# Other homes for the buffers of a hybrid encoder layer: mixer, output projection and MLP on one core of Trainium2

## The chip, the core and the metric

The kernel runs on one core of one Trainium2 chip. The metric is device microseconds of one launch on that core; the time before is the median of 3 runs. The core has five engines that run side by side, each with its own queue of instructions: TensorE (PE in the rows) multiplies matrices out of SBUF into eight PSUM banks, VectorE (DVE), ScalarE (ACT) and GpSimd (POOL) work on tiles of up to 128 partitions, and SyncE (SP) here issues all the DMA transfers between HBM and SBUF.

## The reference, cut to what matters

One encoder layer over T = 2048 tokens of width 1024, in float32, with 256 memory tokens:

```
h = rmsnorm(x, norm_mix_w)
q, k, v, z, xbc, dt, qx = split(h @ w_in)      # 512, 128, 128, 1024, 1536, 32, 512 columns
att  = windowed_gqa(rope(rmsnorm(q)), rope(rmsnorm(k)), v, sink)   # 8 heads, 2 kv, +-128 tokens
xbc  = silu(conv5(xbc)); y = ssd(forward) + ssd(backward) + d * xs # 16 heads, chunks of 128
ssd  = rmsnorm(y * silu(z)) per group                              # 2 groups of 512
xatt = cross_attention(rmsnorm(qx), mem @ w_mem_kv)                # 4 heads
x = x + concat(att, ssd, xatt) @ w_out
return x + square(relu(rmsnorm(x, norm_mlp_w) @ w_up)) @ w_down    # inner width 4096
```

## The kernel before, in words

**Products.** A float32 operand is split into two numbers of TensorE's faster float type, hi and lo (`split`: ACT makes hi, DVE or POOL makes lo); a product is three matmuls, hi·hi, hi·lo and lo·hi. So every weight and every activation is loaded raw, split, and kept twice (names ending in h and l, in regions named X, W, A).

**Stages.** Stage 1 runs the tokens in two halves, 1024 to 2047 first ("half one"), then 0 to 1023 ("half two"). In each: `kv_products` loads xT (the transposed x, 8 blocks k of 128 rows), splits it and multiplies by w_kvdt (288 columns) for eight token tiles of 128; then the 12 xbc columns with their convolution, cross attention in four pairs of tiles, and q in four pairs, whose results are transposed in A and stored to q_d. In half two the backward SSD states ("back chunks") lie between them. `z_first` ends stage 1: the eight columns of z for the first 512 tokens. Stage 2 goes over 16 token tiles times 2 groups: an attention unit, an SSD unit and, for the other tokens, one of 24 z columns (`z_col`, 24 matmuls each), with `z_block` loading and splitting xT again for every 512 tokens. Stage 3 takes pairs of tiles through the output projection (`out_pair`: four products of 4 blocks of 128 rows of w_out each) and `mid` (norm, transposes, sums stored to xc_d), and then the MLP, written as seven products of half matrices instead of eight (`ORDER`), weights loaded into wr0 and wr1, combined, and split into wh and wl.

**What sets the order.** The program records all instructions, then `plan()` orders them by a cost model: it keeps the ready instructions of each engine by their place in the recording, takes the engine that can start first (on equal times the first in the list `engs`), hands out the eight PSUM banks, lets eight DMAs be in flight, and lets DVE and POOL use their shared SBUF port one at a time (`port`). The engines' queues are then issued in that order, all from line 390 (391 after the change), so every row has that line; tiles tell the instructions apart.

**Homes.** SBUF is divided into named regions: const, late, small, X0 to X3, W0, W1, A0, A1, B, Z, C, E. `use(region, ...)` gives a region a new set of buffers; each name in it is a ring of so many buffers. Nothing in the new set may be written before every user of the region's previous set is done, whichever of its buffers that was. `memory1()` to `memory4()` are these maps for stage 1, stage 2, the output projection and the MLP. A row's names are regions: `X<-xbc_d` is a load from DRAM into one of X0 to X3.

Of the kernel before, what the change touches and what calls it, by code (L numbers as in the profile page):

```python
# [73 lines left out]
class Program:  # L74
# [193 lines left out]
    def plan(self):  # L268

        engs = ("", "PE", "ACT", "DVE", "POOL", "SP")  # L270
# [131 lines left out]
class Memory:  # L402
# [5 lines left out]
    def use(self, region, dt, **tags):  # L408

        size = {t: -(-n // CELL) * CELL for t, (n, _) in tags.items()}  # L410
        total = sum(size[t] * b for t, (_, b) in tags.items())
# [4 lines left out]
        for t, (_, b) in tags.items():  # L416
            self.tags[t] = (v, at, size[t], b, dt)
            self.count[t] = 0
            at += size[t] * b
# [15 lines left out]
class Hybrid:  # L435
# [53 lines left out]
    def constants(self):  # L489
# [28 lines left out]
        self.load(cols, a["cols"])  # L518
# [33 lines left out]
    def memory1(self):  # L552
# [8 lines left out]
        m.use("B", F32, pre=(1030, 2), cacc=(1026, 2), stg=(1024, 2), tm=(512, 3), bbt=(256, 2))  # L561
        m.use("Z", F32, raw=(1024, 2), rrow=(1024, 1), vd=(160, 1), rp_u=(128, 1))
        m.use("C", F32, state=(1024, 2), vm=(1024, 1), rp_w=(128, 1))

    def memory2(self):
        m = self.mem
        m.use("X0", F32R, zxh=(512, 8))
        m.use("X1", F32R, zxl=(512, 8))
        m.use("A0", F32R, zwh=(1024, 2), zwl=(1024, 2))
        m.use("Z", F32, zwr=(1024, 1), zraw=(512, 2), zrow=(512, 1), zt=(512, 2))  # L570
        m.use("A1", F32R, sr=(1024, 2), kw=(768, 2))
        m.use("E", F32R, mv=(1024, 2), qs=(512, 2))
        m.use("X2", F32, xb=(1536, 2), y=(512, 2))
        m.use("X3", F32, ap=(1536, 2), ao=(256, 2))
        m.use("W0", F32, fr=(1024, 2), bk=(1024, 2))
        m.use("W1", F32, pb=(1024, 2), ee=(1024, 2))
        m.use("B", F32, xs=(1280, 2), sf0=(512, 2), sf1=(512, 2), apT=(1536, 2))
        m.use("C", F32, vw=(192, 2), zth=(512, 2), xw=(512, 2))

    def memory3(self):  # L580
        m = self.mem
        for i, (h, l) in enumerate((("X0", "X1"), ("late", "A1"), ("X2", "X3"), ("W0", "W1"))):
            m.use(h, F32R, **{f"woh{i}": (1024, 4)})
            m.use(l, F32R, **{f"wol{i}": (1024, 4)})
        m.use("A0", F32R, ah=(512, 4), al=(512, 4))
# [5 lines left out]
    def memory4(self):  # L591
        m = self.mem
        m.use("X0", F32R, xr0=(2048, 2))
        m.use("X1", F32R, xr1=(2048, 2))
# [124 lines left out]
    def kv_products(self, pool, t0, tts, w, ps):  # L719

        nc, a = self.nc, self.a
        if not w:
            self.xh, self.xl = [], []
        rings = ("cacc", "cacc", "pre", "pre", "stg", "stg", "cacc", "cacc")
# [409 lines left out]
    def z_first(self, pool):  # L1134
# [167 lines left out]
    def stage2(self):  # L1302
# [337 lines left out]
def layouts(inp):  # L1640
# [61 lines left out]
```

## Time and profile before

| what | value |
|---|---|
| median of 3 runs | 2861.55 us (2851.22 to 2866.41) |
| profiled execution | 2861.82 us, span 2859.8 us |
| busy share of the span | PE 97%, DVE 66%, ACT 48%, POOL 19% |
| mean granted clock of TensorE | 0.989 |
| chain that ended last | PE 81%, DVE 6%, DMA 6%, ACT 4% |
| DMA | 510.27 MB, mean 178 GB/s |

The span runs from the first to the last instruction. An engine's busy share says how much of the span it worked, not whether it was late; the chain says who held up the end, step by step. TensorE's idle time, 2859.8 less 2760.0, is short and lies in few places, so the rows below look at stretches: where its busy time is less than the stretch, and where the clock that it was granted is below 1.00. In a timeline row the bracket at the end is the idle time before it and what released it.

### The profile page before, as it was taken

The page shows a single profiled execution, that of the slowest core. Times are in us where ns is not written, and L with a number is a line of the kernel's source. Part 1 is how long each engine was busy: PE and PEld are TensorE (multiplying, and loading weights), DVE is VectorE, ACT ScalarE, POOL GpSimd, SP SyncE. Part 2 cuts the span into 40 slices and gives each one's busy share as a digit, 9 for nine tenths or more (in the row PEclk, how much of TensorE's full clock was granted, in tenths as well). Part 3 has the DMA queues.
Part 4 walks back from the last instruction along what each step waited for, and adds up shares of the span by engine and source line. Part 5 has one row for each costly group of instructions (what it writes and reads, how often), then busy time and mean ns, then how long its engine had stood idle before and what let it go on. Part 6 is the DMA issues. An engine that isn't in the chain of part 4 may idle for free.

```text
span 2859.8 us, 37348 instructions
## 1 busy us (share of the span) xinstructions
PE 2760.0 (97%) x13628; PEld 2254.6 (79%) x13628; DVE 1899.3 (66%) x3115; ACT 1359.1 (48%) x2276; POOL 544.7 (19%) x488
## 2 busy tenths in 40 slices
PE   8999979999889999999999899999999999999999
PEld 7788767787667777768888788888888888888887
DVE  6874558855567766666767577584848585766756
ACT  5545534353457676663333363444435353535352
POOL 2302424426254544431101000000000000000000
PEclk9999989999999999999999999999999999999999
DMA  6561335634597877775555691726344653626251
GB/s 212 174 201 60 110 118 170 192 100 155 190 293 223 261 238 234 213 240 190 208 178 204 241 343 56 239 85 204 121 157 165 240 181 111 199 96 221 77 174 59
DMA packets 283691, 510.27 MB, mean 178 GB/s; under 512 B 35954, under 2 KB 124402, under 8 KB 283508
## 3 DMA queue, kind: packets, MB, share of 16 engines
q1 hardware_dynamic: 283508, 507.89, 54.1%
q8 instruction: 108, 1.77, 0.3%
q14 instruction: 75, 0.61, 0.1%
HBM read 390.36 MB, written 117.45 MB: 178 GB/s over the span
## 4 chain that ended last, share of the span: by engine, by line
PE 81%; DVE 6%; DMA 6%; ACT 4%; issue 2%; POOL 1%; SPq 0%; ACTq 0%; POOLq 0%; DVEq 0%
PE bank L390 81%; DVE B L390 2%; ACT X L390 2%; DVE X L390 1%; ACT B L390 1%; DVE small L390 1%; DVE A L390 1%; DMA Z<-in_x_dram 1%; ACT W L390 1%; DMA B<-in_xT_dram 1%; DMA Z<-in_w_out_dram 1%; ACT A L390 1%; POOL B L390 1%; DVE W L390 1%; POOL W L390 0%
## 5 line engine op out<-in xcount | busy, mean ns | idle before, releaser
L390 PE MATMUL bank<-X,X 128*128 128x512 f32 x2688 | 611.0, 389 | 2.0 <-DVE X L390 2.0
L390 PEld LDWEIGHTS bank<-X,X 128*128 128x128 f32 x2688 | 504.6, 188 | 106.9 <-DVE X L390 2.4
L390 PE MATMUL bank<-X,E 128*128 128x512 f32 x1792 | 551.7, 389 | 0.0
L390 PEld LDWEIGHTS bank<-X,E 128*128 128x128 f32 x1792 | 336.4, 188 | 69.8
L390 PE MATMUL bank<-X,W 128*128 128x512 f32 (+1 forms) x1584 | 367.0, 381 | 8.0 <-ACT W L390 3.1
L390 PE MATMUL bank<-X,A 128*128 128x512 f32 x1344 | 350.3, 406 | 11.8 <-ACT X L390 8.3
L390 PE MATMUL bank<-X,C 128*128 128x512 f32 x896 | 348.5, 389 | 0.0
L390 PEld LDWEIGHTS bank<-X,W 128*128 128x128 f32 x1584 | 286.3, 191 | 67.7 <-issue 6.0
L390 PEld LDWEIGHTS bank<-X,A 128*128 128x128 f32 x1344 | 249.4, 190 | 79.4 <-issue 15.0
L390 PE MATMUL bank<-W,X 128*128 128x512 f32 (+1 forms) x1152 | 253.5, 370 | 12.4 <-ACT X L390 11.3
L390 DVE TENSOR_TENSOR X<-A,X 128x1024 fp32r<-128x1024 f32 x128 | 156.5, 1222 | 122.3 <-ACT X L390 121.6
L390 PEld LDWEIGHTS bank<-W,X 128*128 128x128 f32 x1152 | 195.3, 192 | 43.3 <-ACT X L390 11.7
L390 DVE TENSOR_TENSOR X<-Z,X 128x1024 fp32r<-128x1024 f32 x100 | 123.1, 1232 | 135.1 <-ACT X L390 135.0
L390 DVE TENSOR_TENSOR B<-B,bank 128x512 f32<-128x512 f32 x286 | 189.9, 683 | 34.3 <-PE bank L390 34.1
L390 PEld LDWEIGHTS bank<-X,C 128*128 128x128 f32 x896 | 168.2, 188 | 34.8
L390 ACT CAST X<-A 128x1024 fp32r<-128x1024 f32 x128 | 134.0, 1047 | 117.0 <-PE bank L390 115.7
L390 DVE TENSOR_TENSOR W<-W,bank 128x512 f32<-128x512 f32 x220 | 145.2, 683 | 48.0 <-POOL W L390 25.8
L390 ACT ACTIVATE X<-X,small 128x384 f32<-128x384 f32 (+1 forms) x256 | 143.5, 601 | 62.9 <-DVE small L390 62.8
L390 ACT CAST X<-Z 128x1024 fp32r<-128x1024 f32 x100 | 105.0, 1051 | 132.9 <-PE bank L390 99.6
L390 ACT ACTIVATE W<-W 128x512 f32<-128x512 f32 x224 | 134.1, 627 | 59.8 <-DVE W L390 57.4
L390 POOL TENSOR_TENSOR W<-W 128x512 f32<-128x512 f32 x92 | 119.9, 1314 | 183.6 <-ACT W L390 161.3
L390 ACT CAST E<-W 128x1024 fp32r<-128x1024 f32 x66 | 69.3, 1051 | 166.3 <-PE bank L390 164.5
(169 smaller groups left out, 4031.0 us busy)
## 6 DMA issues: line engine op xcount, KB each, us to landing
X<-xc_d SPq DMA_DIRECT2D x112, 1024.0 KB
A<-in_w_up_dram SPq DMA_DIRECT2D x64, 512.0 KB
A<-in_w_down_dram SPq DMA_DIRECT2D x64, 512.0 KB
xc_d<-E SPq DMA_DIRECT2D x56, 512.0 KB
Z<-in_w_z_dram SPq DMA_DIRECT2D x32, 512.0 KB
W<-erow_d SPq DMA_DIRECT2D x64, 256.0 KB
Z<-in_w_xbc_dram SPq DMA_DIRECT2D x24, 512.0 KB
X<-xbc_d SPq DMA_DIRECT2D x16, 768.0 KB
```

Of the source, the lines that this page charges most:

```text
L390: o.fn(*[fix(x) for x in o.args], **{k: fix(x) for k, x in o.kw.items()})
```

## The change

It has six parts, none of which changes what is computed.

1. The port in turns: in `plan`, when DVE and POOL can start at the same time, the one that did not use the port last comes first.
2. The constants: the table `cols` is loaded in two pieces, the first without the cosines and sines (256 of its 368 columns).
3. Input in halves: `kv_products` loads and splits xT in blocks of 512 tokens instead of 1024, the first block ahead of the second; w_kvdt comes in pieces of 288, 576, 864 and 576 columns.
4. Stage 1 and 2 homes: `use` lets a buffer have a type of its own; zt, vd, bbt and the rope scratch leave B, C and part of Z; most of stage 2's buffers change region.
5. The output projection: ah and al go to X3, wol2 to A0.
6. The MLP: xr0, wr0, wh, wl, xr1, wr1 and us change region.

TensorE's and POOL's instructions are as many as before; the splits of xT are 16 of 512 columns instead of 8 of 1024 in each half, and the DMAs 1230 instead of 1211.

```diff
-        engs = ("", "PE", "ACT", "DVE", "POOL", "SP")
+        engs = ["", "PE", "ACT", "POOL", "DVE", "SP"]
...
             if o.port:
                 port = end
+                engs[3:5] = ("POOL", "DVE") if e == "DVE" else ("DVE", "POOL")
...
-        self.load(cols, a["cols"])
+        first = NCOL - 256
+        self.load(cols[:, :first], a["cols"][:, :first])
...
         yield
+        self.load(cols[:, first:], a["cols"][:, first:])
...
-        m.use("B", F32, pre=(1030, 2), cacc=(1026, 2), stg=(1024, 2), tm=(512, 3), bbt=(256, 2))
-        m.use("Z", F32, raw=(1024, 2), rrow=(1024, 1), vd=(160, 1), rp_u=(128, 1))
-        m.use("C", F32, state=(1024, 2), vm=(1024, 1), rp_w=(128, 1))
+        m.use("B", F32, pre=(1030, 2), cacc=(1026, 2), stg=(1024, 2), tm=(512, 3))
+        m.use("Z", F32, raw=(1024, 2), rrow=(1024, 1), zt=(512, 2))
+        m.use("E", F32, vd=(160, 1), rp_u=(128, 1), rp_w=(128, 1), bbt=(256, 2))
+        m.use("C", F32, state=(1024, 2), vm=(1024, 1))
 
     def memory2(self):
         m = self.mem
+        m.use("E", F32R, mv=(1024, 2), qs=(512, 2))
+        m.use("A1", F32R, sr=(1024, 2), kw=(768, 2), vw=(192, 2, F32))
+        m.use("A0", F32, fr=(1024, 2), xw=(512, 2), ao=(256, 2))
+        m.use("B", F32, xs=(1280, 2), sf0=(512, 2), sf1=(512, 2), xb=(1536, 2))
+        m.use("C", F32, ap=(1536, 2))
         m.use("X0", F32R, zxh=(512, 8))
         m.use("X1", F32R, zxl=(512, 8))
-        m.use("A0", F32R, zwh=(1024, 2), zwl=(1024, 2))
+        m.use("X2", F32, apT=(1536, 2), y=(512, 2))
+        m.use("X3", F32R, zwh=(1024, 2), zwl=(1024, 2))
+        m.use("W0", F32, bk=(1024, 2), pb=(1024, 2))
+        m.use("W1", F32, ee=(1024, 2), zth=(512, 2))
         m.use("Z", F32, zwr=(1024, 1), zraw=(512, 2), zrow=(512, 1), zt=(512, 2))
-        m.use("A1", F32R, sr=(1024, 2), kw=(768, 2))
-        m.use("E", F32R, mv=(1024, 2), qs=(512, 2))
-        m.use("X2", F32, xb=(1536, 2), y=(512, 2))
-        m.use("X3", F32, ap=(1536, 2), ao=(256, 2))
-        m.use("W0", F32, fr=(1024, 2), bk=(1024, 2))
-        m.use("W1", F32, pb=(1024, 2), ee=(1024, 2))
-        m.use("B", F32, xs=(1280, 2), sf0=(512, 2), sf1=(512, 2), apT=(1536, 2))
-        m.use("C", F32, vw=(192, 2), zth=(512, 2), xw=(512, 2))
...
-        for i, (h, l) in enumerate((("X0", "X1"), ("late", "A1"), ("X2", "X3"), ("W0", "W1"))):
+        for i, (h, l) in enumerate((("X0", "X1"), ("late", "A1"), ("X2", "A0"), ("W0", "W1"))):
...
-        m.use("A0", F32R, ah=(512, 4), al=(512, 4))
+        m.use("X3", F32R, ah=(512, 4), al=(512, 4))
...
-        m.use("X1", F32R, xr1=(2048, 2))
-        m.use("A0", F32, wr0=(1024, 4))
-        m.use("A1", F32, wr1=(1024, 4))
-        m.use("X2", F32R, wh=(1024, 4))
-        m.use("X3", F32R, wl=(1024, 4))
+        m.use("X1", F32, wr0=(1024, 4))
+        m.use("late", F32R, wh=(1024, 4))
+        m.use("A1", F32R, wl=(1024, 4))
+        m.use("X2", F32R, xr1=(2048, 2))
+        m.use("A0", F32, wr1=(1024, 4))
...
-        m.use("late", F32, us=(1024, 2))
+        m.use("X3", F32, us=(1024, 2))
...
+    def kv_weights(self, pool, w, n):
+
+        k = len(w)
+        if k % 3 == 0:
+            self.kv_piece = [pool.tile([P, 864], t, r) for t, r in ((F32, "raw"), (F32R, "wh"), (F32R, "wl"))]
+        s = slice(k % 3 * 288, (k % 3 + n) * 288)
+        raw, hi, lo = (t[:, s] for t in self.kv_piece)
+        self.load(raw, self.a["w_kvdt"][k // 3][:, s])
+        self.split(hi, lo, raw)
...
+    def kv_products(self, pool, t0, b, tts, w, ps):
...
+        load = len(self.x_in) < 2 * KT and b == len(self.x_in) // KT
...
+        sb = slice(b * BLK, (b + 1) * BLK)
         for k in range(KT):
+            if load:
+                if k % 2 == 0:
+                    raw2 = pool.tile([P, 1024], F32, ("cacc", "pre", "stg", "cacc", "pre", "stg", "cacc", "pre")[b * 4 + k // 2])
+                raw = raw2[:, (k % 2) * BLK:(k % 2 + 1) * BLK]
+                self.load(raw, self.a["xT"][k, :, t0 + b * BLK:t0 + (b + 1) * BLK])
             if len(w) <= k:
...
+                self.kv_weights(pool, w, 1 if k == 0 else 3 - k % 3 if k < 6 else 2)
+            if load:
+                self.split(self.xh[k][:, sb], self.xl[k][:, sb], raw, self.w_mix[:, k:k + 1])
+                self.x_in.append(k)
...
-            self.kv_products(pool, t0, range(0, 4), wk, pk)
+            self.x_in = []
+            self.kv_products(pool, t0, 0, range(0, 4), wk, pk)
...
+            self.kv_products(pool, t0, 1, (4, 5), wk, pk)
             w0 = self.weights(pool, a["w_xbc"][0], (KT, P))
...
+            self.kvdt_tiles(pool, t0, range(0, 4), pk)
             self.xbc_col(pool, t0, 0, w0)
-            self.kv_products(pool, t0, (4, 5), wk, pk)
-            self.kvdt_tiles(pool, t0, range(0, 4), pk)
-            self.kv_products(pool, t0, (6, 7), wk, pk)
+            self.kv_products(pool, t0, 1, (6, 7), wk, pk)
...
-            self.z_col(pool, 0, c, self.z_weights(pool, c, "w"), "stg")
+            self.z_col(pool, 0, c, self.z_weights(pool, c, "w"), self.r_row[:, BLK:])
...
-        for n, (ts, ring) in enumerate(((self.mv, "fr"), (self.sr, "bk"))):
+        for n, (ts, ring) in enumerate(((self.mv, "fr"), (self.sr, "fr"))):
```

In words for what is cut: `cols` has its parts in another order, so that the cosines and sines stand last; in `z_col` zt always comes from the ring zt and th, the tanh's buffer, from the caller.

Three places in the queues show what the orders make of it. First SyncE's queue where half one ends and half two begins. B is the region of xT's landing buffers, A_0 that of q's transposed results, Z that of raw weights. Before:

```order
L390 DMA q_d<-A_0_99 128x1024 x3
L390 DMA B_100<-in_xT_dram 128x1024
L390 DMA q_d<-A_0_99 128x1024
L390 DMA B_100<-in_xT_dram 128x1024
L390 DMA Z_101<-in_w_kvdt_dram 128x576
L390 DMA q_d<-A_0_99 128x1024
L390 DMA Z_101<-in_w_xbc_dram 128x1024
L390 DMA B_100<-in_xT_dram 128x1024 x2
L390 DMA Z_101<-in_w_xbc_dram 128x1024 x2
L390 DMA q_d<-A_0_99 128x1024
L390 DMA B_100<-in_xT_dram 128x1024
L390 DMA q_d<-A_0_99 128x1024
```

After; four more loads of 512 stand up to 12 rows further ahead:

```order
L391 DMA q_d<-A_0_99 128x1024 x3
L391 DMA B_100<-in_xT_dram 128x512 x2
L391 DMA q_d<-A_0_99 128x1024
L391 DMA B_100<-in_xT_dram 128x512
L391 DMA Z_101<-in_w_kvdt_dram 128x576
L391 DMA B_100<-in_xT_dram 128x512 x2
L391 DMA Z_101<-in_w_xbc_dram 128x1024
L391 DMA q_d<-A_0_99 128x1024
L391 DMA B_100<-in_xT_dram 128x512 x4
L391 DMA Z_101<-in_w_xbc_dram 128x1024
L391 DMA q_d<-A_0_99 128x1024
L391 DMA B_100<-in_xT_dram 128x512
```

Before, the seventh and the eighth load of xT stand behind the sixth and the seventh q_d store. Now the eighth half load (the last of tiles 0 to 3) stands ahead of the fifth q_d store, and the last of the second half, four rows below these, behind the seventh.

Second, TensorE's queue at the end of z_first, whose last matmul is the first row. A_1_5589 and, after, A_1_5699 hold sr and kw, E mv and qs; xb is X_1_5703 before and B_5611 after, and A_1_5039 holds the state product's other operand, xw. Before:

```order
L390 MATMUL bank_82<-X_0_94,W_0_97 128x512
L390 MATMUL bank_81<-A_1_5589,E_104 128x256 x2
L390 MATMUL bank_83<-A_1_5589,E_104 128x256 x2
L390 MATMUL bank_80<-A_1_5589,E_104 128x256 x2
L390 MATMUL bank_84<-A_1_5589,E_104 128x256 x2
L390 MATMUL bank_79<-A_1_5589,E_104 128x256 x2
L390 MATMUL bank_78<-A_1_5589,E_104 128x256 x2
L390 MATMUL bank_77<-A_1_5589,E_104 128x256 x2
L390 MATMUL bank_82<-A_1_5589,E_104 128x256 x2
L390 MATMUL bank_81<-X_1_5703 128x128
L390 MATMUL bank_83<-X_1_5703 128x128
L390 MATMUL bank_80<-X_1_5686,A_1_4937 128x512
```

After:

```order
L391 MATMUL bank_84<-X_0_94,W_0_97 128x512
L391 MATMUL bank_81<-A_1_5699,E_5581 128x256 x2
L391 MATMUL bank_77<-A_1_5699,E_5581 128x256 x2
L391 MATMUL bank_78<-A_1_5699,E_5581 128x256 x2
L391 MATMUL bank_79<-A_1_5699,E_5581 128x256 x2
L391 MATMUL bank_80<-B_5611 128x128
L391 MATMUL bank_83<-E_5581,A_1_5699 128x512
L391 MATMUL bank_82<-E_5581,A_1_5699 128x512
L391 MATMUL bank_84<-E_5581,A_1_5699 128x512
L391 MATMUL bank_81<-E_5581,A_1_5699 128x512
L391 MATMUL bank_77<-A_1_5039,B_5611 128x512
L391 MATMUL bank_83<-A_1_5699,E_5581 128x256 x2
```

The product with xb alone (128x128, pc) moved from behind sixteen score matmuls to behind eight, the mask products (E, A_1, 512 wide) and the state product (A_1, B) follow it, and the first z matmul, the last row of before, comes 25 rows below the last row of after.

Third, TensorE's queue from the end of the last pair of the output projection to the MLP. W_2 is the last weights' region, A_2 or X_2 that of ah and al, const_88 with B the transposes of the last mid, X_3_12041 and X_3_12097 are xr0, X_3_12275 is xr1, and wh is X_3_12219 before and late_12188 after (wl is A_3_12184 there). Before:

```order
L390 MATMUL bank_82<-W_2_9682,A_2_9197 128x512
L390 MATMUL bank_80<-W_2_9682,A_2_9197 128x512
L390 MATMUL bank_83<-const_88,B_9691 128x128 x4
L390 MATMUL bank_79<-const_88,B_9691 128x128 x4
L390 MATMUL bank_78<-const_88,B_9691 128x128 x4
L390 MATMUL bank_77<-const_88,B_9691 128x128 x4
L390 MATMUL bank_84<-X_3_12041,X_3_12219 128x512 x2
```

After, with 48 matmuls cut to their first and last rows:

```order
L391 MATMUL bank_77<-W_2_9729,X_2_9253 128x512
L391 MATMUL bank_83<-W_2_9729,X_2_9253 128x512
L391 MATMUL bank_80<-X_3_12097,late_12188 128x512 x2
L391 MATMUL bank_80<-X_3_12097,A_3_12184 128x512
L391 MATMUL bank_80<-X_3_12097,late_12188 128x512 x2
...
L391 MATMUL bank_82<-X_3_12275,late_12188 128x512 x2
L391 MATMUL bank_82<-X_3_12275,A_3_12184 128x512
L391 MATMUL bank_78<-X_3_12097,late_12188 128x512 x2
L391 MATMUL bank_78<-X_3_12097,A_3_12184 128x512
L391 MATMUL bank_79<-const_88,B_9762 128x128 x4
L391 MATMUL bank_77<-const_88,B_9762 128x128 x4
```

The MLP's first matmuls moved from behind the 16 transposes to ahead of them.

## Rows read from the trace of the kernel before

**Rows 1.** Page's first part: busy us, share of the span, instructions

```profile
PE 2760.0 (97%) x13628; PEld 2254.6 (79%) x13628; DVE 1899.3 (66%) x3115; ACT 1359.1 (48%) x2276; POOL 544.7 (19%) x488
```

**Rows 2.** Windows: stretch, length, busy (count) per engine, clock, DMA share, GB/s

```profile
0.00:10.65 10.65, 0.00 (x0) 0.00 (x0) 2.26 (x5) 3.34 (x3) 2.26 (x13) 1.00 0.79 241
10.65:30.00 19.35, 19.34 (x132) 19.11 (x133) 14.39 (x18) 14.20 (x20) 0.00 (x0) 1.00 0.88 357
60.00:130.00 70.00, 64.38 (x302) 51.56 (x300) 59.91 (x116) 37.90 (x64) 27.57 (x35) 0.98 0.54 164
355.00:385.00 30.00, 17.50 (x87) 14.65 (x87) 20.82 (x47) 12.22 (x17) 6.22 (x9) 0.67 0.57 189
420.00:560.00 140.00, 132.07 (x597) 103.06 (x596) 120.19 (x163) 51.30 (x73) 68.34 (x42) 0.99 0.61 187
770.00:790.00 20.00, 9.80 (x47) 8.06 (x46) 11.34 (x35) 14.15 (x33) 5.20 (x4) 0.66 0.93 302
790.00:835.00 45.00, 39.33 (x249) 28.94 (x248) 32.56 (x64) 27.29 (x57) 25.07 (x19) 1.00 0.95 307
1195.00:1295.00 100.00, 88.65 (x500) 67.86 (x499) 68.95 (x158) 63.16 (x134) 36.85 (x34) 0.93 0.72 235
1620.00:1640.00 20.00, 12.12 (x54) 9.99 (x53) 12.02 (x27) 8.18 (x11) 0.00 (x0) 0.83 0.77 265
1640.00:2860.00 1220.00, 1216.12 (x5366) 1006.98 (x5364) 820.86 (x854) 541.83 (x691) 0.00 (x0) 1.00 0.48 161
```

**Rows 3.** Chain that ended last: start, length in us, what ran

```profile
1.71 7.66 DMA B<-in_xT_dram
9.46 1.16 ACT X L390
...
731.96 5.19 DMA z_d<-B
```

**Rows 4.** Timeline of TensorE, 352 to 395: start, length, instructions, idle before

```profile
352.26 4.18 PE L390 MATMUL bank<-W,X 128*128 128x512 f32 x26
...
362.37 7.11 PE L390 MATMUL bank<-W,X 128*128 128x288 f32 x42 [0.62 <-ACT X L390]
373.12 1.11 PE L390 MATMUL bank<-const,A 128*128 128x128 f32 x4 [3.64 <-DVE A L390]
```

**Rows 5.** Timeline of SyncE's DMA queue, 376 to 379 and 771 to 774

```profile
377.28 0.33 SPq L390 DMA_DIRECT2D q_d<-A  x1
377.66 0.42 SPq L390 DMA_DIRECT2D B<-in_xT_dram  x1
...
771.75 0.38 SPq L390 DMA_DIRECT2D X<-xbc_d  x1
772.23 0.38 SPq L390 DMA_DIRECT2D Z<-in_w_z_dram  x1
...
773.22 0.42 SPq L390 DMA_DIRECT2D z_d<-B  x1
```

**Rows 6.** Timeline of TensorE, 770 to 800

```profile
770.84 2.07 PE L390 MATMUL bank<-A,E 128*128 128x256 f32 x16
778.11 1.19 PE L390 MATMUL bank<-X 128*128 128x128 f32 x4 [5.20 <-DMA X<-xbc_d]
781.42 0.80 PE L390 MATMUL bank<-X,A 128*128 128x512 f32 x1 [2.12 <-ACT X L390]
```

**Rows 7.** Timeline of TensorE, 1598 to 1650

```profile
1631.65 3.58 PE L390 MATMUL bank<-const,B 128*128 128x128 f32 x16 [5.87 <-ACT B L390]
...
1639.08 11.18 PE L390 MATMUL bank<-X,X 128*128 128x512 f32 x48 [2.00 <-DVE X L390]
```

**Rows 8.** Timeline of POOL and DVE, 61 to 63

```profile
62.08 2.45 POOL L390 TENSOR_TENSOR W<-Z,W 128x1024 fp32r<-128x1024 f32 x1 [4.56 <-ACT W L390]
62.25 2.31 DVE L390 TENSOR_TENSOR small<-small 128x8 f32<-128x8 f32 x1
```

**Rows 9.** POOL's groups by line and form: busy, mean ns, idle before, releaser

```profile
L390 POOL TENSOR_TENSOR W<-Z,W 128x1024 fp32r<-128x1024 f32 x38 | 98.6, 2596 | 228.5 <-ACT W L390 228.5
```

More of the change, by code (lines that the diff above doesn't have):

```diff
@@ L408, in use @@
     def use(self, region, dt, **tags):
-        size = {t: -(-n // CELL) * CELL for t, (n, _) in tags.items()}
-        total = sum(size[t] * b for t, (_, b) in tags.items())
+        size = {t: -(-v[0] // CELL) * CELL for t, v in tags.items()}
+        total = sum(size[t] * v[1] for t, v in tags.items())
         k = self.uses[region] = self.uses.get(region, -1) + 1
@@ L415, in use @@
         at = 0
-        for t, (_, b) in tags.items():
-            self.tags[t] = (v, at, size[t], b, dt)
+        for t, (_, b, *own) in tags.items():
+            self.tags[t] = (v, at, size[t], b, (own or [dt])[0])
             self.count[t] = 0
@@ L428, in tile @@
         v = v[:shape[0], at:at + need]
+        if v.dtype != dt:
+            v = v.bitcast(dt)
         axes = "abcde"[:len(shape) - 1]
@@ L716, in mem_kv @@
             self.split(self.kmh[:, :, s], self.kml[:, :, s], pt.rearrange("p (h m) -> p h m", h=4))
[L719 to L724, printed above, removed]
+    def kv_weights(self, pool, w, n):
[6 more added lines that the diff above has]
+        self.split(hi, lo, raw)
+        w += [(hi[:, i * 288:(i + 1) * 288], lo[:, i * 288:(i + 1) * 288]) for i in range(n)]
@@ L725, in kv_products @@
+    def kv_products(self, pool, t0, b, tts, w, ps):
+        if not b and not w:
+            self.xh, self.xl = ([pool.tile([P, 1024], F32R, f"{t}{k}") for k in range(KT)] for t in ("xh", "xl"))
+        load = len(self.x_in) < 2 * KT and b == len(self.x_in) // KT
         for tt in tts:
             ps[tt] = self.ps()
+        sb = slice(b * BLK, (b + 1) * BLK)
         for k in range(KT):
-            if len(w) <= k:
-                n = min(3, KT - k)
-                wh, wl = self.weights(pool, a["w_kvdt"][k // 3][:, :n * 288], (n, 288))
-                w += [(wh[:, i, :], wl[:, i, :]) for i in range(n)]
@@ L1138, in z_first, with z_col @@
         for c in range(8):
-            self.z_col(pool, 0, c, self.z_weights(pool, c, "w"), "stg")
+            self.z_col(pool, 0, c, self.z_weights(pool, c, "w"), self.r_row[:, BLK:])
     def z_weights(self, pool, c, pre="zw"):
         return self.weights(pool, self.a["w_z"][c], (KT, P), pre)
-    def z_col(self, pool, b, c, w, out="zt"):
+    def z_col(self, pool, b, c, w, th=None):
         nc = self.nc
@@ L1153, in z_col @@
             mm(ps, wl[:, k, :], xh[k], start=False, stop=k == KT - 1)
-        zt = pool.tile([P, BLK], F32, out)
-        th = pool.tile([P, BLK], F32, "zth" if out == "zt" else out)
+        zt = pool.tile([P, BLK], F32, "zt")
+        th = pool.tile([P, BLK], F32, "zth") if th is None else th
         nc.vector.scalar_tensor_tensor(zt, ps, 0.5, row, ALU.mult, ALU.mult)
@@ L1696, in layouts @@
     tab = lambda t: c(t.astype(np.float32).reshape(NJ, P, 8).transpose(1, 0, 2))
-    cols = [f[n][0].reshape(8, P).T for n in ("norm_mix_w", "mem_norm_w", "norm_mlp_w", "ssd_norm_w")]
-    cols += [f["conv_w"][0].T.reshape(NXC, P, 5).transpose(1, 0, 2), f["conv_b"][0].reshape(NXC, P).T,
-             np.repeat(f["ssd_d"][0], 64).reshape(8, P).T, tab(np.cos(ang)), tab(np.sin(ang))]
+    per = lambda n: f[n][0].reshape(8, P).T
+    cols = [per("norm_mix_w"), f["conv_w"][0].T.reshape(NXC, P, 5).transpose(1, 0, 2), f["conv_b"][0].reshape(NXC, P).T,
+             per("mem_norm_w"), per("norm_mlp_w"), per("ssd_norm_w"), np.repeat(f["ssd_d"][0], 64).reshape(8, P).T, tab(np.cos(ang)), tab(np.sin(ang))]
     o["cols"] = np.concatenate([t.reshape(P, -1) for t in cols], axis=1)
```

10 lines of the change are left out of this document (1 added, 9 removed).

## Prediction

> **What bounds the kernel now.** I read the page's first part first: TensorE is busy 2760.0 us, 97% of the span [rows 1]. Then the table by stretches, where the reader should subtract TensorE's busy time from each stretch's length and look at the granted clock [rows 2]. The MLP, from 1640 us on, is solid: 1216.12 busy of 1220, 5366 matmuls, 0.227 us each. No edit can win there. So everything that homes for buffers can give back lies in the 96 us of idle before it (2859.8 - 2760.0, less 3.9 at the end), and in work done at the lower clock. It is concentrated:
>
> - 0 to 10.65: 10.65 idle, nothing has arrived.
> - 355 to 385 (token half one ends, half two begins): 12.5 idle, clock 0.67.
> - 770 to 835 (stage 1 to stage 2): 10.2 + 5.67 = 15.9 idle, clock 0.66 in its first 20 us.
> - 1195 to 1295 (stage 2 to 3): 11.35 idle, clock 0.93.
> - 1620 to 1640 (stage 3 to the MLP): 7.88 idle, clock 0.83.
>
> Together 58 us; the rest is spread thin, most of it at 60 to 130 and 420 to 560, where DVE is busy 59.91 of 70 and 120.19 of 140. The timelines of TensorE and of the DMA queue then say which wait ends each gap.
>
> The sum is made against the profiled execution, 2861.82 us (2.0 of it outside the span); the median of three runs is 2861.55, so the two can be exchanged. A difference under 0.5%, 14 us, cannot be told from none.
>
> **The start.** First the time: the first xT load takes 7.66 us and ACT's split 1.16, then TensorE starts [rows 3]. Ahead of that start stand 184 KB of cols, 432 of w_kvdt and 512 of xT; now it is 56 + 144 + 256. That is 672 KB less at the 241 GB/s of this stretch [rows 2], 2.9 us, and half of ACT's 1.16: 3.4 us earlier. What is late next: DVE. Its column work needs r_row, hence all eight rows of x, whose bytes and place behind xT don't change, and DVE is what TensorE waits for from 60 on. Bounds 3.4 and -2 (16 splits instead of 8 on ACT and DVE); I take 1, nearer to the DVE-bound row.
>
> **Half one to half two.** After q's last five products (of the 26 matmuls from 352.26) TensorE has 21 matmuls of 288 columns, waits, and has 42 more from 362.37; then it waits 3.64 us for the last q pair's transposes [rows 4]. The rest of half two is not there: its last xT load is issued at 377.66, behind a q_d store that went at 377.28 [rows 5]. The loss is 12.5 idle, plus the clock: a mean of 0.67 is two thirds of 30 us at 1.2 GHz, so about 11.6 of the 17.5 busy us cost double what they should, 5.8. Together 18.3.
>
> Now the order has all eight first-half loads before the fifth q_d store, and tiles 0 to 3 need only these. Ahead of the last 16 transposes TensorE has 96 matmuls of 288 columns, at 0.147 us (19.34 us for 132 at 10.65 to 30 [rows 2]) 14.1, and nine of xbc column 0, at 0.227 2.0. From some 353.5 that reaches 370, against transposes ready at 373.1; behind them stand 48 more of 288 columns (7.1 us) and 14 of 512 (3.2) before k = 7 of the second half must be there, which still stands behind the seventh q_d store. I leave 5 of the 18.3 (3 for the transposes, 2 for k = 7) and take 13. Bounds: 17, and 4 if ACT and DVE, with 16 splits to do and no less q work, release the last pair no earlier and the second half comes late as a whole.
>
> **Stage 1 to stage 2.** T0 is 770.84, when z_first's last matmul has run. Before, both attention units' 16 score matmuls take 2.07 us; then come 5.20 for xb's DMA and 2.12 for the first z block's split [rows 6]. xb could not be loaded before T0, because its region X2 held the second half's x; nor the masks (pick) or ap. The change puts xb into B, pick's landing place into A0, ap into C, and z_first's scratch out of B: all free before T0. So pc, the products of sr and mv and the state product follow the scores at once. The loss is 15.9 idle plus the clock: at 0.66 two thirds of the 9.80 busy us, so 3.3; 19.2 together.
>
> What is late next, two things. pb is still in W0, free at T0. The xbc load, issued at 771.75, released TensorE at 778.11, 6.4 us [rows 5, 6]; pb is smaller, and about 3 us of ready work covers it, so 3 remain. And z: zt now lies in Z, so Z changes hands only when the last z_d store has landed, not at T0. The last store goes 2.4 after T0 (773.22) and a z_d store takes 5.19 [rows 3, 5]; then the same 9.2 from the w_z load's issue (772.23) to the first z matmul (781.42): T0 + 16.8 against T0 + 10.6. The order puts 65 small products ahead of it, 8.5 us at the 0.13 of the score matmuls, some 10 with those of 512 columns; with pb's wait that is T0 + 13, 4 more idle. I leave 10, a part of it for ACT, which has the same splits and exponentials to do, and take 9. Bounds: 15, and 0.
>
> **Stage 2 to 3.** ah and al go to X3, wol2 to A0; both homes are as free as before, and the waits there are for w_out behind a ring of two in Z. Zero, bounds 3 and -4.
>
> **Stage 3 to the MLP.** TensorE waits 5.87 for the last mid's scaling and 2.00 for the first weight split [rows 7]. wr0 lay in A0, held by ah and al to the last product. Now wr0, wh and wl lie in X1, late and A1, whose last readers are products 0 and 1 of the last pair; 48 MLP matmuls, 10.9 us at 0.227, now precede the 16 transposes, and cover the DVE and ACT chain behind which these wait. xr1, needed after 24 of them, is in X2, free after product 2. I take the 7.88, and 1 for the clock (0.83 over 20 us: a third at half, of 12.1 busy 4, half of that is 2): 9. Bounds 10 and 4.
>
> **Port in turns.** It does no work; it reorders a few neighbours on each engine wherever the planner met DVE and POOL at the same moment. Zero, bounds +6 and -6, as only the order moves.
>
> Sum: 1 + 13 + 9 + 0 + 9 + 0 = 32. 2861.8 - 32 = 2830.
>
> The trace has xT in 512 KB loads at 357 GB/s at 10.65 to 30, and 256 KB pieces among others at 302 to 307 at 770 to 835 [rows 2]. The Trainium skill (DMA: Bandwidth & Descriptors, section Bandwidth) advises batches of 1 MiB, since smaller ones reach less of the peak, which speaks against halves. By it xT's 4.2 MB would take 13.8 us instead of 11.8 in each half, the sum would be 28 and the time 2834; the trace cannot part size from mixture here.
>
> **Rivals.**
> 1. *The second half's gain is handed back.* DVE is busy 86% at 420 to 560, TensorE idle 8. If DVE sets the pace there, coming 13 us early only lengthens its waits. Against it: DVE's own work there hangs on the same products and starts earlier too. 2861.8 - 9 - 9 = 2844. Chance 0.13.
> 2. *That, and z's late home eats the transition.* If z's block, 6 us later than before, is what TensorE runs out of, the 9 are gone too: 2861.8 - 9 = 2853, no measurable change. Chance 0.13.
> 3. *Slower, by the port.* At 62.08 POOL's weight split held 2.45 us, and a DVE instruction on 8 columns that started inside it took 2.31 [rows 8]. There are 38 such POOL splits of 2.6 us [rows 9]. If turns let POOL in just ahead of DVE's evacuations, each costs TensorE up to 2.2 us. Two thirds of them, 25 x 2.2 = 55, turn 2830 into 2885; from 21 collisions on, the kernel is measurably slower. Against it: before, POOL already got in by itself, and DVE's order around the evacuations stays nearly the same. Chance 0.05. The Trainium skill (SBUF — State Buffer, section SBUF: two separate sides) calls the shared pair an exclusive lock, kept for the whole instruction, with the loser fully blocked; the two rows agree, and by that the planner's turns decide nothing but who is asked first.
>
> **How the numbers follow.** Forecast 0.62 (its own range 2820 to 2840), rival 1 0.13, rival 2 0.13, rival 3 0.05, better than forecast (no clock drops left, residues smaller) 0.07. Faster by over 0.5%, under 2847: forecast, the better case and most of rival 1, 0.79; within it 0.16; slower 0.05. The range is 2812 to 2851: the better case below, rival 1 and most of rival 2 above.
>
> **What would show it.** First matmul near 7 us; TensorE at 355 to 385 idle by under 6 and the clock near 1; no wait for xb's DMA after z_first, but waits for pb (W0) and for the first z block; no idle at the seam to the MLP, whose matmuls run ahead of the last transposes; 420 to 560 no more idle than the 8 us of before. The forecast is wrong if TensorE's busy time plus idle moved from the seams to 60 to 130 or 420 to 560, or if evacuations on DVE grew longer beside POOL.

## The result, and the profile after

The changed kernel takes 2826.66 us (median of 4 runs, 2824.23 to 2829.05) against 2861.02: ratio 0.9885, 95% interval 0.9867 to 0.9903. Forecast were 2830. The profiled execution took 2824.23 us, span 2822.4. The page's first part after, against [rows 1]:

```profile
PE 2758.7 (98%) x13628; PEld 2251.5 (80%) x13628; DVE 1882.9 (67%) x3133; ACT 1361.1 (48%) x2294; POOL 554.1 (20%) x488
```

TensorE's work is the same (2758.7 against 2760.0); what went is idle time and low clock. The stretches of the changed kernel that answer to [rows 2], in the same columns; the last four are shifted by 27 to 30 us, about as far as the changed kernel is ahead there:

```profile
0.00:10.65 10.65, 2.58 (x11) 2.58 (x12) 4.15 (x8) 4.95 (x8) 2.26 (x13) 1.00 0.79 259
355.00:385.00 30.00, 26.46 (x171) 24.71 (x171) 18.97 (x65) 12.81 (x30) 9.83 (x26) 0.94 0.38 132
420.00:560.00 140.00, 134.69 (x613) 105.38 (x612) 124.52 (x152) 51.95 (x71) 69.88 (x41) 1.00 0.59 178
743.00:763.00 20.00, 14.35 (x100) 11.00 (x98) 14.87 (x42) 9.39 (x20) 12.81 (x11) 0.96 0.94 297
763.00:808.00 45.00, 41.59 (x227) 30.64 (x228) 28.11 (x74) 31.72 (x78) 13.90 (x11) 0.90 0.91 287
1166.00:1266.00 100.00, 86.78 (x468) 65.17 (x467) 66.68 (x146) 61.70 (x130) 35.74 (x34) 0.90 0.67 223
1590.00:1610.00 20.00, 20.00 (x95) 16.48 (x94) 17.36 (x29) 10.16 (x14) 0.00 (x0) 1.00 1.02 389
```

At the seam of the halves 3.5 idle are left in this stretch (5.2 with the part of the same waits that lies ahead of it) and the clock is 0.94; at the seam to the MLP there is none; stage 1 to 2 is down from 15.9 idle to 9.1 (5.7 + 3.4). Stage 2 to 3 has grown from 11.35 to 13.2 idle, at 0.90. TensorE's timeline after shows what ends the waits that remain, beside [rows 3, 4, 6, 7]:

```profile
8.07 4.21 PE L391 MATMUL bank<-W,X 128*128 128x288 f32 x16 [8.07 <-ACT W L391]
...
358.52 9.74 PE L391 MATMUL bank<-W,X 128*128 128x288 f32 x60 [4.77 <-ACT X L391]
...
751.04 0.50 PE L391 MATMUL bank<-E,A 128*128 128x512 f32 x1 [1.35 <-DVE W L391]
...
762.84 3.29 PE L391 MATMUL bank<-X,X 128*128 128x512 f32 x6 [3.78 <-DVE X L391]
...
1608.31 1.66 PE L391 MATMUL bank<-const,B 128*128 128x128 f32 x12
...
1632.37 0.70 PE L391 MATMUL bank<-X,late 128*128 128x512 f32 x2 [0.84 <-DMA X<-xc_d]
```

Two of these are as the prediction had them: the first z block is late (3.78 idle, 19.05 after z_first's end at 743.79), and TensorE does not wait for the last transposes. Two others are not the waits that it named. The 1.35 is a wait for a PSUM bank, held by a product on DVE that itself waited for the load of ee (from erow_d into W1). The eight matmuls with pb had run before it without a wait:

```profile
747.36 1.05 PE L391 MATMUL bank<-B,W 128*128 128x128 f32 x8
...
750.30 0.69 DVE L391 TENSOR_TENSOR W<-W,bank 128x512 f32<-128x512 f32 x1 [1.37 <-DMA W<-erow_d]
```

And the 4.77 is a wait for the input of tiles 0 to 3. The sixteen half loads of half two don't go in the order of k. In the planner's order those of tiles 0 to 3 come as k = 4, 5, 0, 1 and 2 ahead of the fifth q_d store, and as k = 6, 7 and 3 behind it, tenth to twelfth of the sixteen. So it isn't true, as was said ahead of the prediction, that the eighth half load is the last of tiles 0 to 3. TensorE ran the 36 matmuls of k = 0 to 2 and then stood until the twelfth split, which waited for its load:

```profile
357.75 0.72 ACT L391 ACTIVATE X<-B,const 128x512 fp32r<-128x512 f32 x1 [1.55 <-DMA B<-in_xT_dram]
```

**Leads.** A span tells only the sum. So the tables below give the lead: at equal work of TensorE (each matmul counted by the median spacing of its shape), how many us earlier a kernel's profiled execution is than that of before. The last column is the difference of the spans.

| kernel | median us, ratio | start | end of half one | past the halves' seam | end of stage 1 | z block's seam | last tiles | last output pair | end |
|---|---|---|---|---|---|---|---|---|---|
| changed | 2826.66, 0.9885 | 2.6 | 6.8 | 19.1 | 27.0 | 33.2 | 36.0 | 28.9 | 37.4 |
| a_again | 2825.33, 0.9874 | 2.5 | 5.1 | 16.9 | 24.8 | 33.1 | 35.9 | 25.8 | 34.8 |
| u1_port | 2842.13, 0.9947 | 3.0 | 4.8 | 16.5 | 15.0 | 20.7 | 18.2 | 17.5 | 25.3 |
| u2_halves | 2833.42, 0.9919 | 2.7 | 8.2 | 7.3 | 20.9 | 30.3 | 32.3 | 18.4 | 27.2 |
| u3_mixer_homes | 2839.35, 0.9936 | 3.0 | 8.2 | 21.0 | 28.1 | 28.7 | 26.6 | 18.6 | 27.2 |
| u4_mlp_homes | 2836.18, 0.9931 | 3.1 | 4.1 | 17.0 | 22.2 | 30.1 | 33.7 | 25.1 | 24.2 |
| b1_port | 2859.03, 1.0004 | 1.3 | 8.5 | 8.2 | 21.0 | 21.0 | 14.9 | 7.0 | 6.8 |
| u5_ah_home | 2825.12, 0.9890 | 3.5 | 7.3 | 20.7 | 26.1 | 34.9 | 32.7 | 24.9 | 33.5 |
| f1_ar4 | 2828.15, 0.9896 | 3.3 | 7.0 | 19.0 | 23.5 | 33.1 | 30.2 | 21.2 | 30.8 |
| f2_z_early | 2827.91, 0.9903 | 3.6 | 8.8 | 21.0 | 27.6 | 33.6 | 36.7 | 25.3 | 34.6 |
| f5_turns_stage1 | 2825.38, 0.9881 | 2.9 | 8.6 | 21.0 | 21.3 | 25.1 | 24.4 | 24.1 | 33.6 |
| f8_turns_tile14 | 2819.56, 0.9856 | 3.0 | 6.8 | 19.4 | 26.0 | 35.4 | 36.5 | 34.0 | 43.2 |
| b2_turns_stage1 | 2839.87, 0.9930 | -0.2 | 6.3 | 5.6 | 19.7 | 19.6 | 22.8 | 22.2 | 22.4 |

Eight of these (all but u1, u2, u3, b1 and b2) run the same stage 1 (TensorE's matmuls stand in the same order up to its end), and there their leads are 21.3 to 27.6, mean 24.8: so much does one execution tell. Steps from one column to the next are steadier where they carry a verdict below.

### The profile page after: what moved, and what is told of

It reads as the page before. It is cut to its first block, busy times and chain, and to the rows that moved or that the text cites. A ratio compares the mean times of both kernels' runs of the same rounds, so it can differ in the third digit from the quotient of the medians.

```text
span 2822.4 us, 37441 instructions
## 1 busy us (share of the span) xinstructions
PE 2758.7 (98%) x13628; PEld 2251.5 (80%) x13628; DVE 1882.9 (67%) x3133; ACT 1361.1 (48%) x2294; POOL 554.1 (20%) x488
## 4 chain that ended last, share of the span: by engine, by line
PE 73%; DMA 4%; ACT 3%; DVE 1%; POOL 1%; issue 1%; SPq 0%; ACTq 0%; DVEq 0%; POOLq 0%
PE bank L391 73%; DMA Z<-in_xT_dram 1%; ACT C L391 1%; ACT X L391 1%; DVE X L391 0%; DMA Z<-mix_d 0%; DMA X<-xc_d 0%; ACT B L391 0%; DMA E<-z_d 0%; DMA Z<-in_w_out_dram 0%; DMA B<-x_d 0%; POOL B L391 0%; DMA Z<-in_w_z_dram 0%; ACT A L391 0%; ACT W L391 0%
## 5 line engine op out<-in xcount | busy, mean ns | idle before, releaser
L391 PE MATMUL bank<-X,late 128*128 128x512 f32 x1792 | 552.2, 389 | 0.8 <-DMA X<-xc_d 0.8
L391 PE MATMUL bank<-A,E 128*128 128x512 f32 (+2 forms) x1152 | 401.1, 379 | 0.7 <-DVE W L391 0.7
L391 PE MATMUL bank<-X,A 128*128 128x512 f32 (+1 forms) x1264 | 398.4, 393 | 1.3 <-ACT X L391 1.3
L391 PEld LDWEIGHTS bank<-X,late 128*128 128x128 f32 x1792 | 336.3, 188 | 70.9 <-issue 1.2
L391 PE MATMUL bank<-late,E 128*128 128x512 f32 x896 | 348.5, 389 | 0.0
L391 PE MATMUL bank<-late,C 128*128 128x512 f32 x896 | 348.5, 389 | 0.0
L391 PE MATMUL bank<-X,X 128*128 128x512 f32 x1216 | 326.2, 405 | 12.0 <-ACT X L391 8.2
L391 PE MATMUL bank<-X,W 128*128 128x512 f32 x1344 | 327.2, 398 | 0.0
L391 PEld LDWEIGHTS bank<-X,X 128*128 128x128 f32 x1216 | 225.3, 189 | 72.9 <-ACT X L391 13.9
L391 PEld LDWEIGHTS bank<-A,E 128*128 128x128 f32 x1152 | 212.2, 188 | 41.8 <-issue 2.5
L391 PEld LDWEIGHTS bank<-late,E 128*128 128x128 f32 x896 | 168.2, 188 | 34.9
L391 PEld LDWEIGHTS bank<-late,C 128*128 128x128 f32 x896 | 168.2, 188 | 34.9
```

Source lines behind the costliest of these rows:

```text
L391: o.fn(*[fix(x) for x in o.args], **{k: fix(x) for k, x in o.kw.items()})
```

## Experiments

**u1_port**, the changed kernel without the turns:

```diff
-        engs = ["", "PE", "ACT", "POOL", "DVE", "SP"]
+        engs = ("", "PE", "ACT", "DVE", "POOL", "SP")
...
-                engs[3:5] = ("POOL", "DVE") if e == "DVE" else ("DVE", "POOL")
```

> The changed kernel with the turns at the port undone (DVE always asked before POOL at equal times). Theory: turns only reorder neighbours; the time stays that of the changed kernel, 2827 within 5 us, and TensorE's lead over the kernel before keeps its shape: some 7 us at the end of half one, 22 after the seam of the halves, 36 before stage 3, 30 after it, 38 at the end. Rival 1: the 5 us of lead that half one gained without being forecast come from the turns: 2832, lead at the end of half one 2. Rival 2: the 6.5 us lost between stage 2 and stage 3 come from the turns: 2820, lead still 36 after it.

2842.13, interval of the ratio 0.9929 to 0.9966: 15 us of the gain go with two lines that I had priced at nothing. The theory falls. Most of the loss lies in half two (from 16.5 to 15.0, where the changed kernel goes from 19.1 to 27.0), and 5.3 more between the z block's seam and the last tiles (20.7 to 18.2, against 33.2 to 36.0). Rival 1 accounts for 2 us at most (4.8 at the end of half one, against a mean of 6.8 of the eight). Rival 2 holds at its place: 0.7 lost between stage 2 and 3 instead of 7.1.

**u2_halves**, whole loads of xT and the old order of half one's products:

```diff
-                self.load(raw, self.a["xT"][k, :, t0 + b * BLK:t0 + (b + 1) * BLK])
+                self.load(raw, a["xT"][k, :, t0:t0 + HALF])
...
-            self.kv_products(pool, t0, 0, range(0, 4), wk, pk)
+            self.kv_products(pool, t0, range(0, 4), wk, pk)
```

> The changed kernel with the input in whole loads of 1024 tokens again and the old order of half one's products; homes, constants and port as changed. Theory: the 15 us of the seam between the halves go, all the rest stays: 2841, TensorE idle by about 12 us between half one and half two at a mean clock near 0.67. Rival 1: half one's unforecast 5 us go too (they come from the first half of tiles being finished earlier): 2846. Rival 2: the new homes alone let half two's loads run ahead, the halves are not needed: 2828.

2833.42 (0.9895 to 0.9943), 7 us lost, not 15. At the seam the theory holds: 0.9 lost there, where all nine kernels with halves gain 11.7 to 13.4. The stretch of this kernel, clock and all, against [rows 2]:

```profile
345.00:375.00 30.00, 17.34 (x93) 15.06 (x93) 21.28 (x48) 13.98 (x20) 6.21 (x9) 0.74 0.58 186
```

But half two then gives it 13.6 (7.3 to 20.9), against 5.5 (19.3 to 24.8) for the mean of the eight: about 8 of the seam's 13 us are handed back before stage 1 ends.

**u3_mixer_homes**, memory1 to memory3, z_first, z_col and stage2 as before:

```diff
-        m.use("B", F32, xs=(1280, 2), sf0=(512, 2), sf1=(512, 2), xb=(1536, 2))
+        m.use("X2", F32, xb=(1536, 2), y=(512, 2))
...
-        m.use("X3", F32R, ah=(512, 4), al=(512, 4))
+        m.use("A0", F32R, ah=(512, 4), al=(512, 4))
```

> The changed kernel with the homes of stage 1, stage 2 and the output projection as before (z's first columns in B again); halves, port, constants and the MLP's homes as changed. Theory: the 9 us between stage 1 and 2 are lost, and the 6.5 us lost between stage 2 and 3 come back, because the second pair of splits of the output projection then stands behind the last exponentials in ScalarE's queue: 2829. Rival 1: the loss at stage 2 to 3 stays, since any move of stage 2 in time shuffles that place: 2836. Rival 2: the homes of stage 2 are worth nothing by themselves, the lead at the seam is the second half's: 2827 with the lead at stage 3 still 36.

2839.35 (0.9914 to 0.9958), 13 us lost: rival 1, by more. The waits of [rows 6] are back, and a third behind them:

```profile
749.49 1.20 PE L391 MATMUL bank<-X 128*128 128x128 f32 x4 [4.72 <-DMA X<-xbc_d]
...
753.47 0.79 PE L391 MATMUL bank<-X,A 128*128 128x512 f32 x1 [2.79 <-ACT X L391]
...
756.85 1.19 PE L391 MATMUL bank<-X,W 128*128 128x128 f32 x4 [2.58 <-DMA W<-pb_d]
```

The seam gains 0.6 instead of the 3.8 to 9.6 of the nine kernels with stage 2's new homes, and 8.0 are still lost between stage 2 and 3: the homes are not the cause there.

**u4_mlp_homes**, memory4 as before:

```diff
-        m.use("X1", F32, wr0=(1024, 4))
-        m.use("late", F32R, wh=(1024, 4))
+        m.use("X1", F32R, xr1=(2048, 2))
+        m.use("A0", F32, wr0=(1024, 4))
...
```

> The changed kernel with the MLP's homes as before (the output projection's stay changed, so that wr0's old region A0 is held by a weight until the third product, and wl's X3 by the activations until the last). Theory: the 8.7 us between the output projection and the MLP are lost: 2835, TensorE idle about 8 us before the first MLP matmul, which follows the last 16 transposes. Rival: the wait before the MLP is that of the last norm, whatever the homes: 2827.

2836.18 (0.9909 to 0.9954): the theory's number. From the last output pair on it loses 0.9, where the nine kernels with the MLP's new homes gain 7.8 to 9.6. The wait isn't at the place expected, though: TensorE starts the MLP early and then stands for the operand that the last mid stores and the MLP loads, of which 0.84 were left in the changed kernel:

```profile
1643.53 11.77 PE L391 MATMUL bank<-X,X 128*128 128x512 f32 x42 [6.90 <-DMA X<-xc_d]
```

**b1_port**, the kernel before with the turns alone (the two lines of u1_port, the other way):

> The kernel before with the turns at the port alone added. In ScalarE's queue the second pair of splits of the output projection's activations now stands ahead of the last exponentials of stage 2, as in every kernel with the turns. Theory: the turns are worth some 8 to 10 us in half two (380 to 580 us) and 3 at the start of stage 2, as undoing them in the changed kernel showed, and cost 6 to 8 between stage 2 and stage 3, where ScalarE waits for a DMA with exponentials behind it: about 2853, lead near 11 before stage 3 and near 4 after it. Rival 1: the turns pay only where the input in halves has filled half two: 2861 or more. Rival 2: the loss between stage 2 and 3 is not theirs: 2849.

2859.03 over 10 runs, 0.9993 to 1.0016: no change, between the theory and rival 1. The leads say why: 21.0 by the end of stage 1, more than twice what I expected, of which 6.1 go in stage 2 and 7.9 between stage 2 and 3. (The profiled execution, 2854.81, is the fastest of the ten, so its 6.8 at the end are more than the median has.) Rival 2 falls, and rival 1's reason too: the turns pay without the halves.

**u5_ah_home**, memory3 as before:

```diff
-        m.use("X3", F32R, ah=(512, 4), al=(512, 4))
+        m.use("A0", F32R, ah=(512, 4), al=(512, 4))
```

> The changed kernel with the output projection's homes as before: ah and al in A0, which stage 2 now uses to its end, wol2 in X3. All four splits of the first activations then stand behind the last exponentials in ScalarE's queue. Theory: no exponential waits for a DMA any more, the lead stays near 36 up to the last tile, but the first product of the output projection can't be drawn ahead among stage 2's last matmuls: TensorE waits some 4 to 8 us for the splits at the seam instead, 2826 in all, 3 either way. Rival 1: the wait behind the splits is the whole loss: 2820. Rival 2: the loss has nothing to do with the place of these splits: the same loss plus the late product, 2833.

2825.12 (0.9875 to 0.9904), the time of the changed kernel, as the theory said; but 7.8 are lost between stage 2 and 3 all the same, with one wait of 7.7 us behind POOL at the late first product. By itself it settles nothing on the splits.

**f1_ar4**, four landing buffers for the activations:

```diff
-        m.use("Z", F32, raw=(1024, 2), ar=(512, 2))
+        m.use("Z", F32, raw=(1024, 2), ar=(512, 4))
```

> The changed kernel with four landing buffers for the output projection's activations instead of two, so that the second pair of loads needn't wait for the first pair's splits; the splits stand where they stood in ScalarE's queue, ahead of the last exponentials. Theory: the wait of ScalarE for the second load (2.0 us) goes, and with it 2 to 5 of the 6.5 us: 2823. Rival 1: the work of the splits itself is what comes ahead, not the wait: 2826, as the changed kernel. Rival 2: the earlier loads push back stage 2's own loads: 2830.

2828.15 (0.9877 to 0.9915), 9.0 lost at the place: no gain. ScalarE's waits behind those loads, in us, times and longest, of this kernel and of the changed one:

```profile
ACT X L391 <- DMA Z<-mix_d: 3.5, 2, 2.9
```

```profile
ACT X L391 <- DMA Z<-mix_d: 4.4, 2, 2.5
```

The wait hardly shrank, so the run doesn't take it away as meant; that the splits' wait is the loss is neither shown nor excluded by it.

**f2_z_early**, z's landing buffers where they are free at once:

```diff
-        m.use("W1", F32, ee=(1024, 2), zth=(512, 2))
+        m.use("W1", F32, ee=(1024, 2), zwr=(1024, 1), zraw=(512, 2))
...
-        m.use("Z", F32, zwr=(1024, 1), zraw=(512, 2), zrow=(512, 1), zt=(512, 2))
+        m.use("Z", F32, zrow=(512, 1), zt=(512, 2), zth=(512, 2))
```

> The changed kernel with z's raw weights and raw x of stage 2 landing in W1, which is free when the last of z's first columns has its matmuls, and the tanh's buffer in Z, which waits for the stores of z. Theory: the first z matmul comes some 6 us earlier after the end of stage 1 (19 us after it now) and TensorE's wait of 3.8 us ahead of it goes, with a part of the low clock: 2822. Rival: other waits at the seam (ScalarE's splits and exponentials) take its place: 2826.

2827.91 (0.9888 to 0.9918): the rival. The first z matmul comes 7.81 us after stage 1's end instead of 19.05 (751.06 less 743.25), and TensorE then waits for ScalarE's split of a later block:

```profile
743.25 1.11 PE L391 MATMUL bank<-A,E 128*128 128x256 f32 x8
...
751.06 0.50 PE L391 MATMUL bank<-X,X 128*128 128x512 f32 x1 [0.41 <-ACT X L391]
...
769.24 5.18 PE L391 MATMUL bank<-X,X 128*128 128x512 f32 x12 [5.70 <-ACT X L391]
```

The four kernels that follow ran on one chip, where the kernel before took 2859.54 (7 runs).

**f5_turns_stage1**, the changed kernel with the turns in stage 1 alone (b2 has the same edit on b1):

```diff
-                engs[3:5] = ("POOL", "DVE") if e == "DVE" else ("DVE", "POOL")
+                engs[3:5] = ("POOL", "DVE") if e == "DVE" and i < self.turns else ("DVE", "POOL")
...
     k.stage1()
+    k.nc.turns = len(k.nc.ops)
```

> The changed kernel with the turns at the port kept for stage 1's instructions and DVE always first from stage 2 on. Theory: the turns earn their 12 us in half two and cost 6 between stage 2 and 3, where they mix the last two units' exponentials in ScalarE's queue: lead 27 at the end of stage 1, no loss over 2 us between stage 2 and 3; at the start of stage 2 the turns gave up to 3, which go: 2821 to 2824. Rival 1: the turns gave 6 at the start of stage 2 with the new homes, so nothing is won: 2827. Rival 2: the loss between stage 2 and 3 comes with any kernel that is early there: 2830 or more.

2825.38 (0.9866 to 0.9895), the changed kernel's time. It loses 0.3 between stage 2 and 3, which refutes rival 2, and gains 3.1 over stage 2 where the changed kernel gains 9.0: rival 1's exchange.

**f8_turns_tile14**, the turns up to tile 14 of stage 2:

```diff
         for j in range(NJ):
+            if j == NJ - 2:
+                nc.turns = len(nc.ops)
```

> The changed kernel with the turns kept up to the first 14 of stage 2's 16 tiles, DVE first after that. Theory: lead 36 before the last tiles as in the changed kernel, a loss under 2 us after them, the MLP's 8.7 on top: 2821. Rival: the loss is not the turns' in the last tiles but the order that they leave behind (the two units already interleaved): 2827.

2819.56 (0.9840 to 0.9871): the theory's time. All its runs (2814.13 to 2820.81) lie below all of a_again's (2821.01 to 2826.89), by 0.2 us at the nearest. At the place it loses 2.5, a little over the 2 that I allowed.

**a_again**:

> The changed kernel itself once more, on the same chip as the other three: 2827 within 3 us; its profile shows the same lead at the seams within 3 us (7, 19, 27, 36, 29, 38).

2825.33 (0.9858 to 0.9891). Its leads lie up to 3.1 us from those of the changed kernel's other profiled execution; the last two (25.8 and 34.8, for 29 and 38) miss my 3 us by 0.2.

**b2_turns_stage1**:

> The kernel before with the turns in stage 1 alone, nothing else changed. Theory: the turns' gain of 21 us up to the end of stage 1 stays whole when stage 2 is left as it was: 2840, lead 19 to 21 from the end of stage 1 to the end. Rival: stage 2 with the old homes takes 8 to 10 of it back because it is late at its own start (xb, masks, z), whatever the turns do there: 2850.

2839.87 (0.9915 to 0.9945): the theory, to the microsecond. Two lines and a bound on them give 20 us on the old homes, with nothing else changed: 6.5 in half one and 14.1 in half two. What TensorE waited for from half two to the end of stage 1 (380 to 770 before, 374 to 751 here: the same work), before:

```profile
PE bank L390 <- DVE A L390: 5.4, 5, 2.3
PE bank L390 <- POOL B L390: 3.8, 3, 1.9
PE bank L390 <- DVE B L390: 3.4, 3, 2.0
PE bank L390 <- ACT A L390: 2.9, 2, 2.1
PE bank L390 <- ACT B L390: 1.3, 1, 1.3
```

and with the turns in stage 1:

```profile
PE bank L391 <- ACT A L391: 3.3, 4, 2.1
PE bank L391 <- DVE B L391: 2.3, 1, 2.3
PE bank L391 <- POOL B L391: 0.5, 1, 0.5
```

16.8 us in 14 waits became 6.1 in 6; those behind DVE and POOL, which share the port, fell from 12.6 to 2.8. In about the same work u1, with the halves but without the turns, has 12.1 behind these two (374 to 755), and the changed kernel 5.7 (361 to 743).

**The last tiles.** The same 330 to 335 matmuls in four kernels (stretch and columns as above): before, the changed kernel, b1 (before with turns) and f8.

```profile
1201.00:1255.00 54.00, 49.31 (x335) 37.20 (x334) 37.92 (x106) 44.81 (x109) 25.02 (x21) 0.94 0.71 218
```

```profile
1165.00:1225.00 60.00, 52.55 (x332) 38.66 (x331) 40.29 (x107) 45.72 (x109) 26.73 (x21) 0.89 0.66 208
```

```profile
1186.00:1247.00 61.00, 53.87 (x332) 38.38 (x331) 40.01 (x107) 45.82 (x109) 26.89 (x21) 0.89 0.66 207
```

```profile
1165.00:1222.00 57.00, 51.31 (x330) 37.45 (x329) 38.04 (x105) 44.65 (x109) 26.43 (x20) 0.91 0.66 207
```

With the turns there, 3 to 5 us more busy time (the clock) and 2.5 more idle. Across all runs: the nine profiled executions with turns in the last tiles lose 7.1 to 13.9 from there to the last output pair, the three without 0.3 to 0.7 (u1, f5, b2), f8 2.5. So the turns cost it. How, is argued. ScalarE's queue differs in the same way: where the turns hold, the second pair of splits of the output projection's activations stands ahead of the last exponentials, and those of the last two units (384 and 256 wide) alternate more; in before, u1, f5 and b2 these two splits stand behind them; in f8 one stands ahead and one behind. But u5 has both behind, loses 7.8 all the same, and has a late product of its own there. No run isolates it.

## Why the prediction was right, and where it was not

The time and the sign hold, and four of six terms within their bounds. That the total fits so well is in part luck: two terms that I set to zero were wrong with opposite signs.

- **Start**, 1 (3.4 to -2): TensorE starts 2.6 earlier, of which some 1.5 are left at 52 us. Right.
- **Half one to half two**, 13 (17 to 4): 11.7 to 13.4 in nine kernels, -0.9 to -0.3 in three without the halves. Right in size and place. The reading of the queue was wrong: five of the eight half loads of tiles 0 to 3 stand ahead of the fifth store, not all, and the 5 us that I left for the transposes and k = 7 were in fact 4.77 for k = 3 of these tiles. Rival 1's mechanism, which I gave 0.13, is there too, but only beside the turns. With the halves and without the turns (u1) half two hands back 1.5. With the turns it gives 13.6 (u2), 12.8 (b1) and 14.1 (b2) where the halves are missing and 5.5 where they are there, so about 8 us are a gain that both changes make. Why they overlap, no run shows.
- **Stage 1 to 2**, 9 (15 to 0): 6.2 at the seam, 3.8 to 9.6 over nine kernels, and 0.6 without the homes (u3). Within its bounds, but under the 9. The changed kernel gains 2.8 more to the last tiles, and these aren't the homes' alone: with the homes and without the turns in stage 2, u1 loses 2.5 and f5 0.7 there, with the turns and the old homes u3 loses 2.1. No wait for pb came, for which I had left 3. Ahead of the first z matmul 94 matmuls (13.4 us) stand in the trace, where I had counted 65 and some 10 us, and z came 2.2 us later than reckoned, so that its wait is near my 4 all the same. That z's home is late mattered less than I thought: with it early, ScalarE takes its place (f2).
- **Stage 3 to the MLP**, 9 (10 to 4): 8.5, and 7.8 to 9.6 over nine kernels. Right, and as argued: MLP matmuls run without a gap up to the last transposes.
- **Port in turns**, 0 (6 to -6): wrong. Undone, it costs 15 us, and alone in stage 1 it gives 20. The old kernel gains 6.5 and 7.2 by it in half one already (b2, b1). The failed step is the sentence that it "reorders a few neighbours on each engine wherever the planner met DVE and POOL at the same moment". I took a tie for rare. But an instruction that finds the port taken is put back to the moment at which it falls free, and that is the moment at which the other engine is free as well. If that one has another instruction ready, the meeting ends in a tie, and the list's first engine, DVE, won all of these. Counted in the planner's own run, 195 of POOL's 484 instructions were put back in the kernel before, 105 of them more than once, one 25 times; in the changed kernel 27 more than once, none over 7 times. DVE pays for it: 118 of its instructions are put back more than once, against 46 before. That TensorE waits less for POOL's and DVE's products in half two is what the waits above show.
- **Stage 2 to 3**, 0 (3 to -4): wrong, -7.1 and -10.1 in two executions, through the same turns.
- **Slower, by the port** (rival 3): excluded. DVE's busy time fell from 1899.3 to 1882.9, and of its 208 instructions on 8 columns, 18 took over 1 us, against 17 before.

In the leads of the changed kernel's profiled execution (the medians are 34.4 apart): 2.6 start, 4.2 in half one, 12.3 seam, 7.9 in half two, 9.0 stage 1 to the last tiles, -7.1, 8.5 to the end: 37.4. In my sum the second, the fourth and the sixth are missing: 4.2 + 7.9 - 7.1 = 5.

## What to carry to other kernels

In a list scheduler, look at how ties are broken before calling a rule of them neutral: where a blocked instruction is retried at the moment that the resource falls free, ties are common, and a fixed order makes the same engine lose them all. The gains of two changes in one stage need not add, as those of the halves and the turns in half two; undo each part from the finished kernel and compare at equal work. Before an order of loads is priced, read from it which load each product needs, not only how many stand ahead of it. A rule that helps one stage may cost in the next: bounding it (f8) took 0.2% less time than the changed kernel, four runs against four on one chip, and 1.4% less than the kernel before.

## What the runs showed of the hardware

Executions are not alike inside: eight with the same stage 1 reached its end 21.3 to 27.6 us ahead of before, though the four runs of the changed kernel agree within 0.2%. In u4 the load of what the last mid had just stored to HBM held TensorE for 6.90 us at the seam to the MLP; in the changed kernel other work covers all but 0.84.
